# Seven products for eight, in one more column group of w_down and in half of the gate's v columns

## The chip, the cores and the metric

The kernel runs on one core of one Trainium2 chip. The metric is device time in microseconds. The kernel before took 2023.43 us as the median of three runs (2023.22 to 2023.98).

## What is computed

Two layers over 256 tokens of width 2048, all in fp32. Cut to what matters here:

```
for l in range(DEPTH):                                  # DEPTH = 2
    h = rms_norm(x, norm1_g[l])
    z = h @ w_in[l]                                     # 2048 x 5120
    q, k, v, gu, gv = jnp.split(z, splits, axis=-1)     # 1024 columns each
    q, k = rotary(q), rotary(k)
    attn = dilated_attention(q, k, v)                   # 8 heads of 128
    gm = chunked_gmlp(gelu(gu), gelu(gv), ...)          # 8 groups of 128: layer norm of gv, 128x128 mixing
    x = x + concat([attn, gm]) @ w_out[l]               # 2048 x 2048
    h2 = rms_norm(x, norm2_g[l])
    x = x + square(relu(h2 @ w_up[l])) @ w_down[l]      # 2048 x 8192, 8192 x 2048
```

`gv` is "the gate's v half" of the change. Its layer norm (one per group of 128 columns) feeds a 128x128 product per group, the spatial product.

## The kernel before

**Precision.** Every large product runs on TensorE as three passes of a rounded type: weights and activations are each split into `hi` (the rounded value) and `lo` (the rest), and hi·hi, lo·hi and hi·lo are summed in PSUM. A weight tile ("sub") is 1024 numbers for each of 128 partitions. SP's queue loads it as `raw` (7 buffers); ScalarE (ACT) rounds it to `hi` at line 168 (6 buffers); VectorE (DVE) takes `lo = raw - hi` at line 178 (6 buffers); PE multiplies. The high and low parts of an activation pair come from `to_half` (ACT line 646, DVE line 649).

**Three forms of product.** `transposed` (line 410) keeps the weights stationary and moves 256 tokens: 24 matmuls of 256 columns for one sub. `natural` (lines 470 to 472) keeps the activations stationary and moves 512 weight columns: 12 matmuls of 512 columns for one sub; v and gv come out of it with tokens on the partitions. `fast` (line 440) is a Strassen-Winograd step over 1024 rows and 512 columns, with 2x2 blocks of weights and of activations: seven block products for eight. It has two steps (p = 0, 1) of 42 matmuls of 256 columns. A step takes two loads and makes four subs of them: `Top` (half a tile), `Bottom`, and two of sums, `upper` and `lower`; before `upper` stands on ACT, DVE makes two differences of the raw tiles, and before `lower` two more (lines 219 to 224). It also needs the activation sums, which `sums` (line 800) makes in place on DVE from `inner`, the unsplit activations, and `parts` turns into hi and lo.

**Order.** The schedule is written out by hand: `steps` is a list, and a loop at the end of the program walks it. `done` counts the subs used up. Ahead of a step's matmuls the loop emits the `hi` of subs up to done+5 and the `lo` of subs up to done+4. `soon(n, f)` puts f in front of the matmuls of the step that is n subs later. `later(n, cost, f)` puts f in a queue that is emptied, within a budget of 1.2 us, at the end of each entry of `steps`; an entry made by `mark` has no matmuls, and the queue is emptied behind it as well. The five engines each work through their own list in the order in which it was emitted.

**The first half of a layer.** v (16 natural steps); then k and q of two heads at a time, k0 q0 k1 q1 k2 q2 k3 q3, four transposed steps each; then gv (16 natural steps), gu (16 transposed steps), and w_out. When a k or q block is complete, `after_qk` turns it (ACT lines 577 and 578, DVE lines 579 to 581). Two steps behind a q block stand `scores` (PE lines 593 and 596; DVE lines 602 and 604; exponentials on ACT line 606), then `normalise` (DVE line 611, ACT line 614), `turn` (PE line 622) and `values` (PE lines 635 and 637). gv is scaled on ACT (line 660), goes through gelu (ACT 490, DVE 493, ACT 494, DVE 667), then statistics (DVE 677, 680), then `layer_norm` on GpSimd (POOL, line 690). `spatial` (PE line 699) stands behind the first step of the second, third and fourth gu blocks and of w_out.

**The second half.** Step groups e = 0 to 8: group e computes the e-th eighth of w_up (16 transposed steps of 24 matmuls) and, against the eighth before it, w_down, some column groups of 512 with `fast`, at the places in `ORDER` and `USUAL`:

```
ORDER = {1: ((7, 10), (13, 14)), 6: ((12, 15), (2, 3), (7, 8)), 7: ((7, 10), (2, 3)), 8: ()}
USUAL = ((7, 9), (2, 3), (13, 14))
```

Each pair is the two steps of one column group, as step numbers inside group e. Group 1 of steps therefore has two column groups by seven products, and the third goes through `transposed`.

Of the kernel before, what the change touches and what calls it, by code (L numbers as in the profile page):

```python
# [61 lines left out]

ORDER = {1: ((7, 10), (13, 14)), 6: ((12, 15), (2, 3), (7, 8)), 7: ((7, 10), (2, 3)), 8: ()}
FINAL = (7, 7, 6)
# [3 lines left out]
HALVES = 5  # L68
BEHIND, BETWEEN = 2, 1
D_SCORES, D_NORM, D_TURN, D_VALUES = 2, 1, 3, 2  # L70

# [20 lines left out]
def trunk(ctx: ExitStack, tc: tile.TileContext, layout, xT, consts, gains, w, b_sp, w_sp, out):  # L92
# [8 lines left out]
    pacc = ctx.enter_context(tc.tile_pool(name="pacc", bufs=1, space=bass.MemoryType.PSUM))  # L101
    paux = ctx.enter_context(tc.tile_pool(name="paux", bufs=4, space=bass.MemoryType.PSUM))

# [31 lines left out]
    def acc_bank(i=None, of=4):  # L135
# [3 lines left out]
        return pacc.tile([P, 512], F32, name=f"acc{i}", tag=f"acc{i}")  # L139

    def aux_bank():
        return paux.tile([P, 512], F32, name="aux", tag="aux")

# [222 lines left out]
    def sums_ready():  # L366
        run_until(lambda: summed[0])
# [45 lines left out]

    def fast(name, l, row0, col0, tiles, slots, fresh, last, done):

# [5 lines left out]
        for p in range(2):  # L421
# [3 lines left out]
            def mm(p=p, top=top, bottom=bottom, upper=upper, lower=lower):  # L425
                if p == 0:
                    o.extend(slots())
                half = tiles[0][0]
                sums_ready()
                extra = sum_parts[0]  # L430
                left, right = slice(0, 256), slice(256, 512)

                calls = []

                def product(n, a, lower_rows, tt, b, cols):
                    for k in range(2):
                        xh, xl = (a[:, 4 * lower_rows + 2 * p + k, i, tt * P:(tt + 1) * P] for i in range(2))
                        hi, lo = b.hi[:, k, cols], b.lo[:, k, cols]
                        for j, (lhs, rhs) in enumerate(((xh, hi), (xh, lo), (xl, hi))):
                            calls.append(lambda k=k, j=j, lhs=lhs, rhs=rhs: pe.matmul(  # L440
                                o[n], lhsT=lhs, rhs=rhs, start=(p == 0 and k == 0 and j == 0 and n in fresh),
                                stop=(n in last and p == 1 and k == 1 and j == 2), skip_group_check=True))
# [32 lines left out]
    def mark(fn):  # L475

        steps.append((None, fn, None))

    def from_hs(k):
# [38 lines left out]
    def layer(l, n1, n2, n3, last):  # L518
# [27 lines left out]
        if l:  # L546
            mark(start)
        mix_a, mix_g = [None], [None]
        qk = {}
# [107 lines left out]
        def after_gv(c, ps):  # L657
            z, u = t32("gz", [2, 512], tag="tmpB"), t32("gu", [2, 512], tag="tmpA")
            for tt in range(2):
                act.activation(z[:, tt, :], ps[tt], AF.Copy, scale=n1.half[:, tt:tt + 1])  # L660

            def then(u, z):
# [6 lines left out]

            gelu(z, u, then)  # L670

        def stats(g0):
# [10 lines left out]
        def layer_norm(g0):  # L683
            y, mv = par["y"], par["mv"]
            r = t32("lr", [2, 4])
            rsqrt(nc.gpsimd, r, mv[:, :, g0:g0 + 4, 1], 1.0, LN_EPS, [2, 4])
            for g in range(4):
                for tt in range(2):
                    yg = y[:, tt, (g0 + g) * P:(g0 + g + 1) * P]
                    nc.gpsimd.tensor_scalar(yg, yg, mv[:, tt, g0 + g, 0:1], r[:, tt, g:g + 1],  # L690
                                            op0=OP.subtract, op1=OP.mult)
            par["normed"] += 4
# [47 lines left out]
        hook(base + d + 6, rope)  # L740
        hook(base + d + 8, shift)
        for j in range(4):
            transposed("w_in", l, 0, KC, AW + j * 256, 256, from_hs, lambda c, ps, j=j: after_qk("k", j, ps))
            transposed("w_in", l, 0, KC, j * 256, 256, from_hs, lambda c, ps, j=j: after_qk("q", j, ps))
        natural("w_in", l, 4 * AW, AW, after_gv)
        transposed("w_in", l, 0, KC, 3 * AW, AW, from_hs, after_gu)
# [34 lines left out]
        def after_up(e):  # L781
            def f(c, ps):
# [7 lines left out]
                act.activation(z, z, AF.Square)  # L790
                to_half(hid[e][0], c // P, z, True)
                if c == 768:
                    summed[0] = False
                    if e == 0:
                        new_shared(F32R)
                        sum_parts[0] = shared[0].rearrange("p (k h t) -> p k h t", k=NH, h=2)
                    later(1, 1.5, sums)
            return f

        def sums():  # L800

            a11, a12, a21, a22 = (inner[:, 4 * k:4 * k + 4, t * P:(t + 1) * P] for t in range(2) for k in range(2))
            vec.tensor_tensor(a22, a21, a22, op=OP.add)
            vec.tensor_tensor(a21, a11, a21, op=OP.subtract)
            vec.tensor_tensor(a11, a22, a11, op=OP.subtract)
            vec.tensor_tensor(a12, a12, a11, op=OP.subtract)

# [4 lines left out]
            for k in range(0, 8, 2):  # L812
                later(0, 0.6, lambda k=k: parts(k))

# [33 lines left out]

        def halves(bank):
            return [bank[:, 0:256], bank[:, 256:512]]  # L850

        held = []
# [17 lines left out]
        def put(e, g, r):  # L870

            src = stage[:, r] if g else stage_one
            nc.gpsimd.dma_start(far[g][:, r], src, **({} if e == max(g, 1) else {"accum_op": OP.add}))  # L873

# [38 lines left out]
        for e in range(9):  # L913
# [3 lines left out]
            if e < 8:  # L917
                up = collect(transposed, "w_up", l, 0, KC, e * 1024, 1024, from_hs, after_up(e), of=2)
            if e:
                w = 512 * len(ORDER.get(e, USUAL))  # L920
                hidden = [hid[e - 1]]
                down = collect(transposed, "w_down", l, (e - 1) * 1024, 8, w, D - w, from_tiles(hidden, NH),
                               lambda c, ps, e=e, w=w: after_down(e, (c + w) // P, ps),
                               apart=last and e == 8, of=2 if e < 8 else 4,
                               cols=None if e < 8 else [c * P for c in LAST])
                for g, at in enumerate(ORDER.get(e, USUAL)):
                    banks = []
                    quick += zip(at, collect(fast, "w_down", l, (e - 1) * 1024, 512 * g, hidden,
                                             (lambda g=g, banks=banks: slots_other(g, banks)) if g else slots_first,
# [146 lines left out]
```

## Time and profile before

| | |
|---|---|
| median of three runs | 2023.43 us |
| profiled execution | 2023.7 us, its span 2021.9 us |
| granted TensorE clock, mean | 0.997 |
| PE / DVE / ACT / POOL busy | 99% / 78% / 60% / 8% |
| HBM | 206 GB/s over the span, DMA engines busy 50 to 90% of a slice |

Busy time of PE is the union of matmuls that overlap each other, so the pace of a stage is read from start to start in the chain of waits, not from the mean duration of a matmul (277 ns for 256 columns). DVE and ACT instructions start some 0.1 us before the one ahead of them is reported as ended. In an answer by lines or by time, `x48` is a count, the first number a start or a sum, and the arrow in square brackets is what ended the idle time before the instruction.

### The profile page before, as it was taken

Reading aid. Unit: us, or ns where it says so; the run is one execution under the profiler, and the core shown is the slowest. Engines: PE = TensorE matmul, PEld = TensorE weight load, DVE = VectorE, ACT = ScalarE, POOL = GpSimd, SP = SyncE. Lnnn points to the kernel's source line nnn. Section 1 sums busy time; section 2 is a strip of 40 time slices with the busy share of each in tenths; the row PEclk is TensorE's granted clock in tenths of the full one; section 3 lists DMA queues with packets and bytes.
Section 4 is the critical chain, followed back from the end, with each engine's and each line's share of the span. In section 5 each row is a group of like instructions: output and inputs, shape, how many; then the busy total and the mean of one; then the engine's idle time right before and its main releaser. Section 6 shows DMA issues by size and latency. Waiting matters only on the chain.

```text
span 2021.9 us, 40716 instructions
## 1 busy us (share of the span) xinstructions
PE 2009.5 (99%) x16810; PEld 1973.4 (98%) x16810; DVE 1579.8 (78%) x1954; ACT 1221.2 (60%) x1613; POOL 156.2 (8%) x200
## 2 busy tenths in 40 slices
PE   9999999999999999999999999999999999999997
PEld 8998999999999999999989989999999999999997
DVE  7566766688888898898856667667888898888985
ACT  7565455566566666665645654556666666667653
POOL 0002300000001000100000032000000000010000
PEclk9999999999999999999999999999999999999998
DMA  9555556566678776866664555565676776777662
GB/s 330 192 167 167 187 189 202 174 229 204 222 219 239 240 225 203 249 215 215 201 215 158 168 187 188 188 199 179 217 229 208 228 236 216 239 220 241 212 215 81
DMA packets 126442, 419.26 MB, mean 207 GB/s; under 512 B 14128, under 2 KB 22064, under 8 KB 126256
## 3 DMA queue, kind: packets, MB, share of 16 engines
q1 hardware_dynamic: 110800, 389.86, 57.2%
q0 software_dynamic: 14304, 23.86, 6.5%
q8 instruction: 131, 2.15, 0.4%
q10 hardware_dynamic: 1152, 2.94, 0.4%
q14 instruction: 55, 0.45, 0.1%
HBM read 394.58 MB, written 22.02 MB: 206 GB/s over the span
## 4 chain that ended last, share of the span: by engine, by line
PE 99%; DVE 0%; ACT 0%; issue 0%; DVEq 0%
PE acc L410 70%; PE acc L440 10%; PE aux L440 8%; PE acc L470 3%; PE acc L472 3%; PE acc L471 3%; PE aux L699 0%; PE aux L635 0%; PE aux L593 0%; PE aux L622 0%; PE aux L994 0%; DVE x L1038 0%; PE aux L596 0%; PE aux L637 0%; PE acc L846 0%; PE aux L539 0%
## 5 line engine op out<-in xcount | busy, mean ns | idle before, releaser
L168 ACT ACTIVATE hi<-raw 128x1024 fp32r<-128x1024 f32 (+1 forms) x817 | 836.9, 1050 | 487.5 <-DVE raw L220 216.2
L178 DVE TENSOR_TENSOR lo<-raw,hi 128x1024 fp32r<-128x1024 f32 (+1 forms) x817 | 965.3, 1214 | 143.4 <-ACT hi L168 140.4
L410 PE MATMUL acc<-hs,hi 128*128 128x256 f32 x5632 | 985.9, 277 | 0.0
L410 PEld LDWEIGHTS acc<-hs,hi 128*128 128x128 f32 x5632 | 857.9, 188 | 0.4 <-issue 0.2
L410 PE MATMUL acc<-hs,lo 128*128 128x256 f32 x2816 | 778.0, 276 | 0.0
L410 PEld LDWEIGHTS acc<-hs,lo 128*128 128x128 f32 x2816 | 528.7, 188 | 0.4 <-issue 0.2
L410 PE MATMUL acc<-half,hi 128*128 128x256 f32 x2688 | 462.2, 276 | 0.0
L410 PEld LDWEIGHTS acc<-half,hi 128*128 128x128 f32 x2688 | 406.7, 188 | 0.0
L410 PE MATMUL acc<-half,lo 128*128 128x256 f32 x1344 | 371.0, 276 | 0.0
L410 PEld LDWEIGHTS acc<-half,lo 128*128 128x128 f32 x1344 | 252.3, 188 | 0.0
L873 POOL DMA_DIRECT2D far<-ar x92 | 74.2, 816 | 1164.4 <-ACT ar L876 563.9
L440 PE MATMUL acc<-hi,shared 128*128 128x256 f32 x768 | 138.4, 276 | 0.0
L440 PEld LDWEIGHTS acc<-hi,shared 128*128 128x128 f32 x768 | 119.2, 188 | 0.0
L440 PE MATMUL aux<-hi,half 128*128 128x256 f32 x528 | 110.6, 276 | 0.0
L440 PE MATMUL acc<-lo,shared 128*128 128x256 f32 x384 | 106.0, 276 | 0.0
L649 DVE TENSOR_TENSOR half<-ar,half 128x512 fp32r<-128x512 f32 x72 | 49.8, 691 | 68.6 <-ACT half L646 68.6
L470 PE MATMUL acc<-hi,hs 128*128 128x512 f32 x256 | 101.8, 398 | 0.0
L472 PE MATMUL acc<-hi,hs 128*128 128x512 f32 x256 | 100.6, 393 | 0.0
L471 PE MATMUL acc<-lo,hs 128*128 128x512 f32 x256 | 100.3, 392 | 0.0
L440 PEld LDWEIGHTS aux<-hi,half 128*128 128x128 f32 x528 | 87.2, 188 | 0.0
L440 PE MATMUL aux<-hi,shared 128*128 128x256 f32 x448 | 80.7, 276 | 0.0
L510 DVE TENSOR_TENSOR x<-x,acc 128x512 f32<-128x512 f32 (+1 forms) x49 | 33.1, 675 | 59.1 <-PE acc L410 57.3
(150 smaller groups left out, 1955.3 us busy)
## 6 DMA issues: line engine op xcount, KB each, us to landing
raw<-in_w SPq DMA_DIRECT2D x731, 512.0 KB, 4.7
far<-ar POOLq DMA_DIRECT2D x60, 256.0 KB, 8.3
far<-ar POOLq DMA_DIRECT2D x32, 128.0 KB, 4.3
ar<-far POOLq DMA_DIRECT2D x12, 256.0 KB, 9.7
raw<-in_w SPq DMA_DIRECT2D x10, 256.0 KB, 5.1
x<-in_xT SPq DMA_DIRECT2D x7, 256.0 KB, 5.9
out<-x SPq DMA_DIRECT2D x7, 256.0 KB, 3.1
shared<-in_b_sp ACTq DMA_DIRECT2D x2, 512.0 KB, 7.7
```

The source lines that it names most:

```text
L168: act.activation(self.h[:, j * m:(j + 1) * m], self.raw[:, j * m:(j + 1) * m], AF.Copy)
L178: vec.tensor_tensor(lo[:, r], self.raw[:, r], self.h[:, r].bitcast(F32), op=OP.subtract)
L410: pe.matmul(o, lhsT=lhs, rhs=xs[:, rhs, :], start=(first and j == 0), stop=(last and j == 2), skip_group_check=True)
L440: calls.append(lambda k=k, j=j, lhs=lhs, rhs=rhs: pe.matmul(o[n], lhsT=lhs, rhs=rhs, start=(p == 0 and k == 0 and j == 0 and n in fresh), ...
L470: pe.matmul(ps, lhsT=xh, rhs=hi, start=(k0 + k == 0), stop=False)
L471: pe.matmul(ps, lhsT=xh, rhs=lo, start=False, stop=False)
L472: pe.matmul(ps, lhsT=xl, rhs=hi, start=False, stop=(k0 + k == KC - 1))
L510: vec.tensor_tensor(xj, xj, ps[j][:, 0:S] if alone else pair(ps)[:, j, :], op=OP.add)
L649: vec.tensor_tensor(t[:, c:c + 2, 1, :], src, t[:, c:c + 2, 0, :].bitcast(F32), op=OP.subtract)
L873: nc.gpsimd.dma_start(far[g][:, r], src, **({} if e == max(g, 1) else {"accum_op": OP.add}))
```

## The change

Two things, each in both layers. First, `ORDER[1]` gets a third pair: in step group 1 the third column group (512 columns of w_down, 1024 rows) now goes by `fast`, at steps 13 and 14, and the other two move to 9, 11 and to 5, 6. For that, half of the activation sums are made earlier (`sums([0])` behind the second block of group 0, whose blocks are taken in another order), and the partial results that wait in DRAM are written first in group 1.

Second, the first 512 columns of gv, over both halves of the 2048 rows, go by `fast`. Their four steps stand among the k and q steps: at plain steps 4 and 7 (in q0) for the upper rows, at 15 (in q1) and 23 (in q2) for the lower. Their activation sums are made from x times gain by `seven_sums` (8 ACT, 4 DVE instructions) and `seven_parts` (four times one ACT and one DVE instruction); for the lower rows these stand in marks in front of plain steps 8 to 12. The result stays in two accumulator banks and two auxiliary banks of PSUM until `gather` adds the seven products up on DVE. Meanwhile k and q use two accumulator banks and the small score block an accumulator bank. The other 512 columns stay natural (8 steps), and the gelu of the first half starts inside them. `layer_norm` of the first half moves from POOL to DVE.

```
-ORDER = {1: ((7, 10), (13, 14)), 6: ((12, 15), (2, 3), (7, 8)), 7: ((7, 10), (2, 3)), 8: ()}
+ORDER = {1: ((9, 11), (5, 6), (13, 14)), 6: ((12, 15), (2, 3), (7, 8)), 7: ((7, 10), (2, 3)), 8: ()}
+SEVEN, AGAIN = ((4, 7), (15, 23)), 8
...
-            s1, s0 = aux_bank(), aux_bank()
+            s1, s0 = aux_bank(), acc_bank(1 - bank_at[0]) if aux_held else aux_bank()
...
+        def seven_sums(rows):
+            if "sums" not in seven:
+                f = tp.tile([P, 2, NH, S], F32, name="plain", tag="half", bufs=2)
+                seven["plain"] = [f[:, i, :, :] for i in range(2)]
+                seven["sums"] = tp.tile([P, NH, 2, S], F32R, name="half", tag="half", bufs=2)
+            f = seven["plain"][rows]
+            for k in range(NH):
+                c = NH * rows + k
+                act.activation(f[:, k, :], x[:, c, :], AF.Copy, scale=g_all[:, n1.g, c:c + 1])
+            strassen_sums(f, 0, 4)
+
+        def seven_parts(rows, k):
+            to_half(seven["sums"], k, seven["plain"][rows][:, k:k + 2, :])
...
+        def gather(o):
+            z = t32("gz", [2, 512], tag="tmpB")
+            p1, p2, p3, p5, p7, p6, p4 = o
+            c11, c12, c21, c22 = (z[:, tt, h * S:(h + 1) * S] for tt in range(2) for h in range(2))
+            act.activation(c12, p1, AF.Copy)
+            vec.tensor_tensor(c11, c12, p2, op=OP.add)
...
+            for tt in range(2):
+                act.activation(z[:, tt, :], z[:, tt, :], AF.Copy, scale=n1.half[:, tt:tt + 1])
...
-            rsqrt(nc.gpsimd, r, mv[:, :, g0:g0 + 4, 1], 1.0, LN_EPS, [2, 4])
+            e = nc.gpsimd if g0 else vec
+            rsqrt(e, r, mv[:, :, g0:g0 + 4, 1], 1.0, LN_EPS, [2, 4])
...
+        hook(base + 13, lambda: seven_sums(0))
+        for k in range(0, NH, 2):
+            hook(base + 14 + k // 2, lambda k=k: seven_parts(0, k))
...
-        natural("w_in", l, 4 * AW, AW, after_gv)
...
+        for i, one in enumerate(plain):
+            if quick.get(i):
+                steps.append(quick[i])
+            if i == AGAIN:
+                mark(lambda: seven_sums(1))
+            if AGAIN < i <= AGAIN + 4:
+                mark(lambda k=2 * (i - AGAIN - 1): seven_parts(1, k))
+            steps.append(one)
+        late = collect(natural, "w_in", l, 4 * AW + 512, 512, lambda c, ps: soon(1, lambda: after_gv(512, ps)))
+        for i, one in enumerate(late):
+            if i == 6:
+                mark(lambda: gate_half(0, seven["z"]))
+            steps.append(one)
```

In the changed program lines 168, 178, 410 and 440 have become 173, 183, 415 and 443; `scores` is at 608 and 611 (PE), 617 and 619 (DVE); the turning of q and k at 592 to 596; `spatial` at 768.

**First place: PE, layer 0, from the last matmul of q0 to the scores of heads 0 and 1.** `acc` is the accumulator of a block, `hi_…`/`lo_…` a weight sub, `hs` the activations, `ar` the tile that holds q and k. Before:

```order
L410 MATMUL acc2_703<-hs_85,hi_632 128x256
L410 MATMUL acc3_829<-hs_85,hi_662 128x256 [waits Activation_49]
...
L410 MATMUL acc3_829<-hs_85,hi_697 128x256 [waits Activation_49]
...
L410 MATMUL acc3_829<-hs_85,hi_697 128x256
L593 MATMUL aux_884<-ar_80 128x256 [waits DVE_49,PE_49]
L593 MATMUL aux_884<-ar_80 128x256
L596 MATMUL aux_885<-ar_80 128x128 [waits PE_49]
```

and now:

```order
L415 MATMUL acc0_793<-hs_85,hi_850 128x256
L415 MATMUL acc1_999<-hs_85,hi_880 128x256 [waits Activation_49]
...
L415 MATMUL acc1_999<-hs_85,hi_880 128x256
L608 MATMUL aux3_1026<-ar_80 128x256 [waits DVE_49]
L608 MATMUL aux3_1026<-ar_80 128x256
L611 MATMUL acc0_1027<-ar_80 128x128 [waits PE_49,Activation_49]
L611 MATMUL acc0_1027<-ar_80 128x128
L415 MATMUL acc1_999<-hs_85,hi_926 128x256
```

Two subs of k1 (662, 697) stood between q0 and its scores; now it is one (880), since the marks in front of plain steps 8 and 9 empty the queue as well.

**Second place: DVE, layer 0, from the turning of q0 to the first fast step in q1.** `mx`, `den` and `ar` belong to the attention, `plain` and `half` to the activation sums. Before:

```order
L579 TENSOR_TENSOR ar<-acc_703,cosR 128x512
L580 TENSOR_TENSOR ar<-ar,sinR 128x512
L581 TENSOR_TENSOR ar<-ar 128x512
L178 TENSOR_TENSOR lo<-raw,hi 128x1024 x2
L602 SCALAR_TENSOR_TENSOR ar<-aux,con 128x512
L604 TENSOR_REDUCE mx<-ar 128x2
L602 SCALAR_TENSOR_TENSOR ar<-aux,con 128x256
L604 TENSOR_REDUCE mx<-ar 128x2
L178 TENSOR_TENSOR lo<-raw,hi 128x1024
L611 RECIPROCAL den<-den 128x4
L178 TENSOR_TENSOR lo<-raw,hi 128x1024
L579 TENSOR_TENSOR ar<-acc_829,cosR 128x512
```

Now, behind the same three instructions (lines 594 to 596), first

```order
L485 TENSOR_TENSOR plain<-plain 128x4x128
L486 TENSOR_TENSOR plain<-plain 128x4x128
L487 TENSOR_TENSOR plain<-plain 128x4x128
L488 TENSOR_TENSOR plain<-plain 128x4x128
L183 TENSOR_TENSOR lo<-raw,hi 128x1024
L664 TENSOR_TENSOR half<-plain,half 128x2x256
L617 SCALAR_TENSOR_TENSOR ar<-aux_1026,con 128x512
L619 TENSOR_REDUCE mx<-ar 128x2
L617 SCALAR_TENSOR_TENSOR ar<-acc_1027,con 128x256
L619 TENSOR_REDUCE mx<-ar 128x2
L183 TENSOR_TENSOR lo<-raw,hi 128x1024
L664 TENSOR_TENSOR half<-plain,half 128x2x256
```

and then

```order
L626 RECIPROCAL den<-den 128x4
L183 TENSOR_TENSOR lo<-raw,hi 128x1024
L664 TENSOR_TENSOR half<-plain,half 128x2x256
L196 TENSOR_TENSOR lo<-raw,hi 128x512
L594 TENSOR_TENSOR ar<-acc_999,cosR 128x512
L595 TENSOR_TENSOR ar<-ar,sinR 128x512
L596 TENSOR_TENSOR ar<-ar 128x512
L664 TENSOR_TENSOR half<-plain,half 128x2x256
L183 TENSOR_TENSOR lo<-raw,hi 128x1024
L224 TENSOR_TENSOR raw<-raw 128x2x256
L225 TENSOR_TENSOR raw<-raw 128x2x256
```

Behind these stand lines 228 and 229 and the `lo` of `upper` and `lower`. Between the turning of q0 and that of k1 there were four `lo` of whole subs and the scores; now there are three, one of a half sub (line 196, `Top`), the scores, four sums and three parts.

**Third place: DVE, layer 0, from the second half's gelu to the first gu block.** `shared` holds the gated values, `mv` their statistics. Now:

```order
L507 SCALAR_TENSOR_TENSOR ar<-ar 128x1024
L183 TENSOR_TENSOR lo<-raw,hi 128x1024
L745 BN_STATS bst<-shared 128x6 x8
L748 BN_AGGR mv<-bst 128x2 x8
L686 SCALAR_TENSOR_TENSOR shared<-ar 128x2x512
L183 TENSOR_TENSOR lo<-raw,hi 128x1024
L349 TENSOR_SCALAR rv<-mv 128x8
L353 TENSOR_SCALAR rt<-rv 128x8
...
L759 TENSOR_SCALAR shared<-shared,mv,lr 128x128 x8
L183 TENSOR_TENSOR lo<-raw,hi 128x1024
L776 SCALAR_TENSOR_TENSOR ar<-acc_2212,nR 128x512
```

Before, at the same place:

```order
L493 SCALAR_TENSOR_TENSOR ar<-ar 128x1024
L178 TENSOR_TENSOR lo<-raw,hi 128x1024
L667 SCALAR_TENSOR_TENSOR shared<-ar 128x2x512
L178 TENSOR_TENSOR lo<-raw,hi 128x1024 x2
L677 BN_STATS bst<-shared 128x6 x8
L680 BN_AGGR mv<-bst 128x2 x8
L178 TENSOR_TENSOR lo<-raw,hi 128x1024
L707 SCALAR_TENSOR_TENSOR ar<-acc_2085,nR 128x512
```

The statistics and the layer norm of the first half have come to stand among the gu steps, on DVE, ahead of the first gu block's own work.

More of the change, by code (lines that the diff above doesn't have):

```diff
@@ L139, in acc_bank @@
         return pacc.tile([P, 512], F32, name=f"acc{i}", tag=f"acc{i}")
+    aux_at, aux_held = [3], set()
     def aux_bank():
-        return paux.tile([P, 512], F32, name="aux", tag="aux")
+        i = next(j % 4 for j in range(aux_at[0] + 1, aux_at[0] + 5) if j % 4 not in aux_held)
+        aux_at[0] = i
+        return paux.tile([P, 512], F32, name=f"aux{i}", tag=f"aux{i}")
     class Sub:
@@ L791, in f, with sums @@
                 to_half(hid[e][0], c // P, z, True)
+                if e == 0 and c == 512:
+                    new_shared(F32R)
+                    sum_parts[0] = shared[0].rearrange("p (k h t) -> p k h t", k=NH, h=2)
+                    later(1, 1.0, lambda: sums([0]))
                 if c == 768:
                     summed[0] = False
[L794 to L797, printed above, removed]
-            return f
[L800 to L806, printed above, removed]
+                    later(1, 1.5, lambda: sums([0, 1] if e else [1]))
+            return f
+        def sums(ps):
+            strassen_sums(inner, 2 * ps[0], 2 * len(ps))
             def parts(k):
@@ L812, in sums @@
             for k in range(0, 8, 2):
-                later(0, 0.6, lambda k=k: parts(k))
+                if k % 4 // 2 in ps:
+                    later(0, 0.6, lambda k=k: parts(k))
         def combine(place, c, banks, o=None):
@@ L917, in layer @@
             if e < 8:
[L918 removed]
+                up = collect(transposed, "w_up", l, 0, KC, e * 1024, 1024, from_hs, after_up(e), of=2,
+                             cols=None if e else (0, 512, 256, 768))
             if e:
```

70 lines of the change are left out of this document (56 added, 14 removed).

## The prediction

> **What bounds it now.** I read the page first: busy times, the chain that ended last by engine, then PE's waits (engine, line, what is waited for: us, times, longest).
>
> ```profile
> PE 2009.5 (99%) x16810; PEld 1973.4 (98%) x16810; DVE 1579.8 (78%) x1954; ACT 1221.2 (60%) x1613; POOL 156.2 (8%) x200
> PE 99%; DVE 0%; ACT 0%; issue 0%; DVEq 0%
> PE aux L328 <- DVE nr L354: 1.2, 1, 1.2
> PE aux L994 <- DVE warm L990: 1.1, 1, 1.1
> ```
>
> PE waits 2.3 us in 2021.9. So matmuls taken away shorten the end one for one, and any wait that the change brings lengthens it one for one. Next come the stages that it touches, in the view by windows (length, then busy time and count of PE, PEld, DVE, ACT, POOL, then clock, DMA share, GB/s): k and q of layer 0, its gu blocks, a whole up/down group of layer 1.
>
> ```profile
> 51.60:149.30 97.70, 97.70 (x832) 96.22 (x831) 61.66 (x81) 55.13 (x92) 0.00 (x0) 1.00 0.55 176
> 198.00:247.90 49.90, 49.90 (x443) 49.90 (x442) 38.76 (x61) 26.89 (x33) 21.06 (x25) 1.00 0.53 170
> 1529.00:1612.00 83.00, 83.00 (x733) 83.00 (x733) 72.78 (x82) 54.73 (x70) 7.08 (x10) 1.00 0.70 226
> ```
>
> DVE is at 63% in k/q, 78% in gu, 88% in the up/down group, and PE waits in none. The k/q and gu stages have the room on average; the change fills it in bursts.
>
> **What it removes from PE.** Pace is read from start to start: the chain (start, length) for 256 columns, the timeline for 512.
>
> ```profile
> 1107.84 10.90 PE acc L410 x96
> 1500.47 4.54 PE aux L440 x40
> 16.20 0.39 PE L470 MATMUL acc<-hi,hs 128*128 128x512 f32 x1
> 31.31 0.39 PE L470 MATMUL acc<-hi,hs 128*128 128x512 f32 x1
> ```
>
> 10.90/96 and 4.54/40 are both 113.5 ns. Between the last two rows lie 66 matmuls, 15.11/66 = 228.9 ns. Per layer the v half loses 8 × 12 = 96 matmuls of 512 (21.97 us) and gains 4 × 42 = 168 of 256 (19.07): −2.90. Group 1's third column group goes from 96 to 84 of 256: −1.36. Together −4.26 a layer, **−8.5 us**.
>
> A rule speaks against this. Were narrow matmuls to carry a fixed price that wide ones don't, 168 narrow could cost more than 96 wide. The Trainium skill, "TensorE: Matmul & The Clock Gate", section "Back-to-back issue gap", gives for a stream 81 ns at 128 columns and 131 at 512; an estimate from it is 98 at 256, and by that the v half would cost 3.8 us more a layer, the group 1.2 less, and the sum below would end at 2039. The trace does not agree: 2 × 113.5 = 227.0 stands against 228.9, with no fixed price in it. I give that outcome no chance.
>
> **What it adds.** Groups by form (total busy, mean ns; then idle time before):
>
> ```profile
> L168 ACT ACTIVATE hi<-raw 128x1024 fp32r<-128x1024 f32 x807 | 830.7, 1055 | 485.8 <-DVE raw L220 216.2 <-PE acc L410 149.4 <-PE acc L472 49.3
> L178 DVE TENSOR_TENSOR lo<-raw,hi 128x1024 fp32r<-128x1024 f32 x807 | 958.7, 1220 | 139.3 <-ACT hi L168 136.2
> L191 DVE TENSOR_TENSOR lo<-raw,hi 128x512 fp32r<-128x512 f32 x76 | 52.0, 684 | 2.1 <-ACT hi L186 2.1
> L220 DVE TENSOR_TENSOR raw<-raw 128x512 f32<-128x512 f32 x76 | 52.6, 692 | 2.6
> L646 ACT ACTIVATE half<-ar 128x512 fp32r<-128x512 f32 x72 | 45.4, 630 | 2.0
> L649 DVE TENSOR_TENSOR half<-ar,half 128x512 fp32r<-128x512 f32 x72 | 49.8, 691 | 68.6 <-ACT half L646 68.6
> ```
>
> A step by seven products turns two loads into 0.68 + 3 × 1.22 + 4 × 0.69 = 7.1 us of DVE instead of 2.4, and 0.63 + 3 × 1.06 = 3.8 of ACT (a half-width row is L646) instead of 2.1.
>
> *Group 1* thereby becomes what the third window shows: up plus three groups by seven and one by eight, 83 us with no wait. Its activation sums are made earlier in parts, and eight more writes go to DRAM from POOL, nearly idle there. I cost it at nothing beyond its gain; uncovered, a late pair of differences would cost 0 to 2 us a layer.
>
> *First rows of the v half* (plain steps 4 and 7, in q0): 2 × 4.7 us of DVE over 16 us in which about 37% of it is free, besides sums made a stage earlier. I put the waits at 0; the tightest `lo` I find has about 0.3 us to spare, so 0 to 1.
>
> *Second rows: q0's end to step 15.* Here the marks stack a burst. Rows of the same work in layer 1 (timeline, and three pieces of the chain):
>
> ```profile
> 262.27 0.91 ACT L287 ACTIVATE hs<-x,cols 128x256 fp32r<-128x256 f32 x2 [2.33 <-DVE x L510]
> 1076.33 0.59 ACT L578 ACTIVATE ar<-acc 64x512 f32<-64x512 f32 x1
> 1076.95 0.69 DVE L579 TENSOR_TENSOR ar<-acc,cosR 128x512 f32<-128x512 f32 x1 [4.37 <-ACT ar L578]
> 1078.27 0.69 DVE L581 TENSOR_TENSOR ar<-ar 128x512 f32<-128x512 f32 x1
> 1081.06 0.86 PE aux L593 x4
> 1081.92 0.44 PE aux L596 x4
> 1081.96 0.69 DVE L602 SCALAR_TENSOR_TENSOR ar<-aux,con 128x512 f32<-128x512 f32 x1 [0.72 <-PE aux L593]
> 1083.41 0.51 ACT L606 ACTIVATE ar<-ar,mx 128x256 f32<-128x256 f32 x1 [3.97 <-DVE mx L604]
> 1084.08 1.21 DVE L178 TENSOR_TENSOR lo<-raw,hi 128x1024 fp32r<-128x1024 f32 x1
> 1085.18 1.04 ACT L168 ACTIVATE hi<-raw 128x1024 fp32r<-128x1024 f32 x1
> 1086.13 1.48 ACT L614 ACTIVATE ar<-ar,den 128x256 f32<-128x256 f32 x4
> 93.19 0.65 PE aux L622 x6
> ```
>
> Two transposed steps of 24 × 113.5 = 2.72 us lie ahead of the scores at 1081.06, so q0 ended at 1075.61. Set that to 0 in the changed order. ACT turns q until 1.3 (row 1076.33), DVE until 3.3 (1076.95 and 1078.27: three of 0.66). The scores now stand one step behind q0, at 2.7: **wait 0.7**. ACT's eight gains go on to 4.7 (two take 0.91 with the tail, 0.41 from start to start), DVE's four sums, at 0.70, to 7.5. Behind these DVE has one `lo` (8.6), a part (9.2) and only then the scores, four operations in 2.12 (1081.96 to 1084.08): 11.3. Before, they came at once. ACT's exponentials (1.77, 1083.41 to 1085.18) end at 12.4, a `hi` and a part's high half at 14.0. DVE: `lo` 12.5, part and reciprocal 14.8, `lo` 15.9. ACT: scaling (1.4) 16.2, `Top` 16.7, part 17.3, `hi` 18.2, and only then the turning of k1, which PE finished at about 13.6, to 19.5. DVE: part 18.0, `Top` 18.6, turning 21.4, last part 22.0, `Bottom` 23.2, four differences 25.9; then `upper` 27.2, `lower` 28.4, each `lo` behind its `hi`.
>
> PE, from 2.7, takes 0.7 of wait, 1.3 of scores (0.86 + 0.44), 0.65 of transposes (93.19) and seven steps behind the first: it reaches step 15 at 21.7 and, unhindered, would end its 4.77 at 26.5. The products from `upper` and `lower` end it; with the last `lo` at 28.4 and the matmuls behind it the step ends at 29.8: **wait 3.3**. The next plain step's `lo` comes at 30.2: **0.35**. Four subs of lead, 4 × 2.72 = 10.9 us, are used up here, since DVE has 22 us of work between 1.3 and 28.4 and stands 5 us for ACT and PE. Together 4.3 a layer; DVE's instructions ready sooner would leave the 0.7, and two orders gone wrong by one `lo` each would make it 6.4.
>
> *Third rows* (step 23, in q2): no marks near it. The queue has room, and I find no wait; the result is gathered five steps later, 14 operations against a window with a third of DVE free.
>
> *Gate.* The first half's gelu moves forward into the natural steps, and its layer norm goes to DVE, ahead of the first gu work. The rows:
>
> ```profile
> 1105.23 0.43 PE aux L635 x2
> 1105.66 0.22 PE aux L637 x2
> 197.37 1.38 ACT L660 ACTIVATE ar<-acc,nhalf 128x512 f32<-128x512 f32 x2 [1.00 <-PE acc L472]
> 198.78 1.06 ACT L490 ACTIVATE ar<-ar 128x1024 f32<-128x1024 f32 x1
> 199.88 1.23 DVE L493 SCALAR_TENSOR_TENSOR ar<-ar 128x1024 f32<-128x1024 f32 x1 [4.95 <-ACT ar L490]
> 202.24 1.32 DVE L667 SCALAR_TENSOR_TENSOR shared<-ar 128x1024 f32<-128x1024 f32 x1
> 205.75 1.63 DVE L677 BATCH_NORM_STATS2 bst<-shared 128x6 f32<-128x128 f32 x8
> 207.30 0.62 DVE L680 BATCH_NORM_AGGREGATE mv<-bst 128x2 f32<-128x6 f32 x8
> 1018.61 0.16 DVE L344 TENSOR_SCALAR rv<-aux 128x2 f32<-128x2 f32 x1 [3.46 <-PE aux L320]
> 1020.86 3.50 DVE L178 TENSOR_TENSOR lo<-raw,hi 128x1024 fp32r<-128x1024 f32 x3
> 57.97 2.16 DVE L543 SCALAR_TENSOR_TENSOR shared<-aux,cols,shared 128x128 f32<-128x128 f32 x8 [2.67 <-PE aux L539]
> ```
>
> Set 0 at q3's end. PE gets through the last values at 26.6 (eight natural steps of 12 × 228.9, 22.0; scores 1.3; transposes 0.65; two rounds of values, each twice 0.43 + 0.22); behind them come a part's two halves (0.6, 0.65), the first half's y (1.2), 29.1. The second half's scaling waits for that buffer (1.4), then Square (1.1), 31.6; DVE's inner step, a `lo`, the statistics (1.55 + 0.55), y, a `lo`, and the root (2.25, from 1018.61 to 1020.86): 40.6. The layer norm on DVE isn't in the trace; nearest is 0.26 an operation (row 57.97). PE reaches the spatial product at 26.6 + 5 × 2.72 = 40.2 and its fourth matmul, 0.66 later, needs the fourth, at 41.7: **wait 0.85**, of 0 (POOL's free, or y 1 us sooner) to 1.6.
>
> **Sum.** −8.5 + 2 × 4.3 + 2 × 0.85 = **+1.8**. The profiled execution took 2023.7, its span 2021.9; 0.27 over the median. So span 2023.7, execution 2025.5, against the median **2025.2**. With the low ends of the waits, 2 × 0.7, it is −7.1: 2016.3. With the high, 2 × (6.4 + 1.6), +7.5: 2030.9.
>
> **Rivals.** *The lead holds (faster).* If ACT doesn't delay DVE in the burst, step 15 costs nothing: 1 us a layer or less remains, −6.5: 2016.9. For it: the third window's DVE does 88% without a wait, with its own bursts of differences. Against: there nothing stands ahead of them that waits for PE; here scores and turning do.
>
> *DVE falls behind in gu (slower).* DVE has 38.8 of 49.9 us there (second window); the change adds statistics 2.1, root 2.25, layer norm 2.1 and a displaced y and `lo` of 2.4 to 47.7, or 96%. If the last layer norm ends over 3 us after PE has reached the spatial product, each following `lo` is as late: 3 us a layer more, 2031.2. Against: the lead of 10.9 us, and ACT is at 54%.
>
> *It doesn't do what it says*: the changed order holds the counted matmuls, so no chance for that.
>
> **Chances.** Within 0.2% (4 us, about what a measurement here tells from no change): 0.47, own range 2020 to 2027.5. Faster 0.30; slower 0.23, which takes in step 15 dearer by an order more. The range 2017 to 2029.5 leaves out a third of the faster case and somewhat under half of the slower, 0.2 together.
>
> **What would show it.** PE's waits in the changed profile: 0.7 us twice at the first scores (line 608), some 3.3 twice at the step by seven in q1 (line 443), 0.85 twice at the spatial product (line 768), and none in group 1. PE's busy count falls by 192 matmuls of 512 columns and rises by 312 of 256. I am wrong if line 443 waits under 1 us a layer, or if waits stand at plain steps of gu.

## The result, and the profile after

The changed kernel takes 2070.01 us (median of 6, 2061.71 to 2074.86), the one before 2023.62: a ratio of 1.0227, 95% interval 1.0207 to 1.0248. It is 46 us slower. The time lies 40 us above the top of the predicted range.

The page of the changed kernel, first its busy times and its chain by engine, then PE's waits:

```profile
PE 2048.3 (99%) x16930; PEld 2016.8 (98%) x16930; DVE 1661.9 (80%) x2108; ACT 1262.1 (61%) x1695; POOL 137.0 (7%) x166
PE 92%; DVE 4%; ACT 2%; issue 1%; DMA 0%; SPq 0%; DVEq 0%; ACTq 0%
PE acc L443 <- DVE lo L183: 2.9, 3, 1.1
PE acc L443 <- ACT hi L173: 1.7, 2, 0.9
PE aux L608 <- DVE ar L596: 1.2, 2, 0.6
PE aux L768 <- DVE shared L759: 0.8, 2, 0.4
```

The new waits sum to 6.6 us in this view, and they stand at the lines that the prediction names. PE is as busy as before, 99%, yet 39 us longer. So the time is neither in the waits nor in more matmuls: the matmuls themselves take longer. The view by windows shows it for 300 us in the step groups of each layer, where both programs run the same mixture. First the kernel before, then the changed one (length, then busy time and count of PE, PEld, DVE, ACT, POOL, then clock, DMA share, GB/s):

```profile
500.00:800.00 300.00, 300.00 (x2645) 300.00 (x2645) 262.31 (x297) 197.73 (x250) 26.52 (x32) 1.00 0.72 225
1500.00:1800.00 300.00, 300.00 (x2646) 300.00 (x2645) 261.86 (x296) 197.77 (x250) 26.25 (x32) 1.00 0.72 225
```

```profile
500.00:800.00 300.00, 300.00 (x2547) 300.00 (x2546) 252.14 (x282) 193.22 (x241) 27.59 (x32) 1.00 0.71 216
1500.00:1800.00 300.00, 300.00 (x2550) 300.00 (x2549) 254.37 (x285) 192.33 (x240) 26.50 (x31) 1.00 0.72 221
```

The granted clock is 1.00 in all four, PE is busy for all of the 300 us, and it starts 2645 matmuls before and 2547 now: 113.4 ns and 117.8 ns each. The busy time cannot show this; the count in a window does. On the page only the mean duration of one matmul moves with it, from 277 ns (line 410) to 280 ns (line 415).

Where the pace turns is seen in PE's timeline of the changed kernel (start, busy time), in step group 1 of layer 0 and at the first transposes of group 6:

```profile
435.39 0.28 PE L415 MATMUL acc<-hs,hi 128*128 128x256 f32 x1
435.77 0.38 PE L443 MATMUL acc<-hi,half 128*128 128x256 f32 x1
...
888.45 0.28 PE L415 MATMUL acc<-half,hi 128*128 128x256 f32 x1
888.57 0.60 PE L937 MATMUL acc<-con,ar 128*128 128x128 f32 x4
888.92 0.37 PE L415 MATMUL acc<-half,hi 128*128 128x256 f32 x1
```

Between 435.39 and 435.77 lies 0.38 us where 0.11 would do: PE waited 0.27 us. From there on it starts a matmul of 256 columns every 117.8 ns, for 453 us, until the four narrow transposes at 888.57; behind them it is 113.4 ns again. These transposes stand among the last steps of group 6, where the third column group is finished: the first of the group's four steps of w_down lies ahead of them. Where the expectations below speak of group 8, these are meant. In layer 1 the same happens from 1462 to 1915. Counted from start to start, some 10,000 matmuls of the profiled execution run at 117.8 ns, against some 230 before; 9,800 x 4.44 ns = 43.5 us.

The chain of waits of the kernel before has the slow pace too, in one longer stretch of each layer, between the scores of heads 0 and 1 and their transposes:

```profile
77.97 2.61 PE acc L410 x23
80.57 0.86 PE aux L593 x4
81.44 0.44 PE aux L596 x4
81.88 11.31 PE acc L410 x96
93.19 0.65 PE aux L622 x6
93.84 3.19 PE acc L410 x28
```

11.31/96 is 117.8 ns; 2.61/23 ahead of it and 3.19/28 behind it are 113.5 and 113.9. The two paces could have been read before the change was run.

The books of the profiled executions, 2069.4 against 2023.7: matmuls -8.5, waits from start to start +10.1, a halved clock in layer 1 +1.7 (last section), slow pace +43.5. That is 46.8 of 45.7.

### The profile page after: what moved, and what is told of

Read it like the earlier page. It is cut to its first block, busy times and chain, and to the rows that moved or that the text cites. A ratio compares the mean times of both kernels' runs of the same rounds, so it can differ in the third digit from the quotient of the medians.

```text
span 2067.6 us, 41171 instructions
## 1 busy us (share of the span) xinstructions
PE 2048.3 (99%) x16930; PEld 2016.8 (98%) x16930; DVE 1661.9 (80%) x2108; ACT 1262.1 (61%) x1695; POOL 137.0 (7%) x166
## 4 chain that ended last, share of the span: by engine, by line
PE 92%; DVE 4%; ACT 2%; issue 1%; DMA 0%; SPq 0%; DVEq 0%; ACTq 0%
PE acc L415 64%; PE acc L443 12%; PE aux L443 8%; PE acc L473 2%; PE acc L475 2%; PE acc L474 2%; DVE lo L183 1%; ACT hi L173 1%; PE aux L768 0%; PE aux L650 0%; ACT plain L714 0%; DVE raw L225 0%; DVE raw L228 0%; DVE raw L229 0%; DMA raw<-in_w 0%
## 5 line engine op out<-in xcount | busy, mean ns | idle before, releaser
L183 DVE TENSOR_TENSOR lo<-raw,hi 128x1024 fp32r<-128x1024 f32 (+1 forms) x829 | 981.9, 1217 | 131.7 <-ACT hi L173 127.3
L415 PE MATMUL acc<-hs,hi 128*128 128x256 f32 x5632 | 1011.5, 280 | 0.0
L415 PEld LDWEIGHTS acc<-half,hi 128*128 128x128 f32 x2560 | 390.4, 188 | 0.0
L415 PE MATMUL acc<-half,lo 128*128 128x256 f32 x1280 | 356.3, 278 | 0.0
L443 PE MATMUL acc<-hi,shared 128*128 128x256 f32 x832 | 154.5, 279 | 0.0
L443 PE MATMUL aux<-hi,half 128*128 128x256 f32 x608 | 129.6, 280 | 0.0
L443 PEld LDWEIGHTS aux<-hi,half 128*128 128x128 f32 x608 | 101.2, 188 | 0.0
L443 PE MATMUL acc<-hi,half 128*128 128x256 f32 x480 | 94.8, 280 | 1.9 <-ACT hi L173 1.7
L443 PE MATMUL aux<-lo,half 128*128 128x256 f32 x304 | 85.0, 280 | 0.0
L443 PEld LDWEIGHTS acc<-hi,half 128*128 128x128 f32 x480 | 77.5, 188 | 2.7 <-ACT hi L173 2.1
```

The source lines that it names most:

```text
L183: vec.tensor_tensor(lo[:, r], self.raw[:, r], self.h[:, r].bitcast(F32), op=OP.subtract)
L415: pe.matmul(o, lhsT=lhs, rhs=xs[:, rhs, :], start=(first and j == 0), stop=(last and j == 2), skip_group_check=True)
L443: calls.append(lambda k=k, j=j, lhs=lhs, rhs=rhs: pe.matmul(o[n], lhsT=lhs, rhs=rhs, start=(p == 0 and k == 0 and j == 0 and n in fresh), ...
```

## Experiments

The theory after the result: PE has two paces for the same stream of 256-column matmuls. A wait inside the stream, however short, can put it into the slow one, and it stays there until something else interrupts the stream. The rivals: the pace belongs to the changed program (its banks of PSUM, its order), or a wait costs just what it lasts and the time is elsewhere.

**One part alone, twice.** The v half's part without group 1's:

```
-ORDER = {1: ((9, 11), (5, 6), (13, 14)), ...
+ORDER = {1: ((7, 10), (13, 14)), ...            # and sums, order of group 0, writes as before
```

> The v half's part of the change alone: group 1 of the steps (its column groups, sums and writes) as before. Pace theory: no wait in group 1, so no slow pace in groups 1 to 7 (33.7 us less) but the one in k, q, gv and gu as in the changed kernel (11 us), and 2.7 us of matmuls and 0.8 of waits come back: about 2038. Rival, the new pool of banks gives the slow pace in the groups: 2070 or more.

Measured: 2036.32 us, ratio 1.0065 (1.0050 to 1.0080). And group 1's part without the v half's (the kernel before with the new `ORDER[1]`, the sums in two parts, the order of group 0 and the writes):

> Group 1's part of the change alone, the v half as before. Pace theory: 24 matmuls fewer (2.7 us), waits of 0.4 us a layer in group 1, and the slow pace from there to group 8, 33.7 us: about 2055. If the short wait doesn't come up without the v half's part: 2021. Rival, the slow pace comes with the v half's banks: 2021 to 2022.

Measured: 2054.89 us, ratio 1.0156 (1.0141 to 1.0172). Both came out as the pace theory worked them out, within 2 us. Group 1's part, which takes 2.7 us of matmuls away, costs 31.6 us by itself. The bank pool of the v half's part is not in that kernel, and the v half's part alone, which has it, starts 2646 and 2645 matmuls in the two windows of 300 us, as the kernel before does. So the pool is not the cause of the slow pace in the groups. The window of group 1's part in layer 0:

```profile
500.00:800.00 300.00, 300.00 (x2549) 300.00 (x2549) 251.46 (x282) 193.82 (x244) 27.62 (x32) 1.00 0.72 219
```

The wait behind it, in the timelines of ScalarE and PE of the same kernel, and then in the view of waits, where it stands with the weight loads (PEld), for this kernel and for the changed one (there the Relu is line 880):

```profile
428.48 1.06 ACT L168 ACTIVATE hi<-raw 128x1024 fp32r<-128x1024 f32 x1 [3.34 <-DVE raw L220]
429.93 1.06 ACT L168 ACTIVATE hi<-raw 128x1024 fp32r<-128x1024 f32 x1 [0.39 <-DVE raw L224]
430.90 0.58 ACT L795 ACTIVATE ar<-acc 128x512 f32<-128x512 f32 x1
...
431.15 0.28 PE L410 MATMUL acc<-hs,hi 128*128 128x256 f32 x1
431.53 0.39 PE L440 MATMUL acc<-hi,half 128*128 128x256 f32 x1
...
PEld acc L440 <- ACT ar L795: 0.6, 2, 0.3
PEld acc L443 <- ACT ar L880: 0.6, 2, 0.3
```

Line 795 is the Relu that reads the finished block's accumulator. It stands in ScalarE's list behind two roundings that waited 3.34 and 0.39 us for VectorE's differences, ends at 431.48, and PE's next matmul by seven, which writes into that bank, starts at 431.53 instead of 431.26. The rows of the matmuls alone do not list this wait; those of the weight loads name it, once in each layer.

**A wait put into the kernel before.** Two matmuls more, into a free bank that ScalarE reads in between:

```
+        def stall():
+            b = acc_bank(2)
+            for j in range(2):
+                pe.matmul(b[:, 0:S], lhsT=hs[:, 0, 0, 0:P], rhs=hs[:, 0, 0, :], start=True, stop=True)
+                if j == 0:
+                    act.activation(warm[:, 0:1], b[:, 0:1], AF.Copy)
```

> The kernel before with two matmuls of 256 columns more behind the ninth plain step of group 1, in both layers, into one free bank; ScalarE reads one column of that bank in between, so that TensorE waits once, 1 to 2 us, for ScalarE. Pace theory: from there to the transposes of group 8 TensorE runs at 117.8 ns, about 3500 matmuls a layer x 4.45 ns = 15.6 us, in both layers 31, and with the waits 2056 to 2060. Rival, a wait costs what it lasts: 2025.5 to 2028.

Measured, eight times: 2025.8, 2025.9 and 2026.2; 2043.7, 2044.1 and 2044.3; 2061.4 and 2062.5. The granted clock is 0.997 or 0.998 in all eight. The median, 2043.88, says little. The time is that of the waits alone, or 18 us more, or 36 more. The profiled execution was one of 2044, and its rows show what the 18 us are (PE's timeline around the wait in layer 0 and in layer 1, and the two windows):

```profile
406.12 0.28 PE L915 MATMUL acc<-hs 128*128 128x256 f32 x1
407.19 0.39 PE L915 MATMUL acc<-hs 128*128 128x256 f32 x1 [0.80 <-ACT warm L917]
...
1425.78 0.28 PE L915 MATMUL acc<-hs 128*128 128x256 f32 x1
1426.86 0.38 PE L915 MATMUL acc<-hs 128*128 128x256 f32 x1 [0.80 <-ACT warm L917]
...
500.00:800.00 300.00, 300.00 (x2547) 300.00 (x2547) 251.91 (x281) 194.12 (x242) 26.41 (x32) 1.00 0.70 216
1500.00:1800.00 300.00, 300.00 (x2645) 300.00 (x2645) 260.98 (x293) 198.97 (x251) 27.08 (x33) 1.00 0.73 227
```

The same program, the same wait of 0.97 us (1.07 and 1.08 less a matmul's time), once in each layer: behind the one PE runs at 117.8 ns to the transposes of group 6 (4075 matmuls x 4.44 ns = 18.1 us), behind the other at 113.4. So a wait does not always bring the slow pace. It lets the pace be drawn anew, and here slow came up 7 times in 16, read from the eight times at 18 us each; only the profiled execution has rows. I had expected it always; that was wrong. Nor is it an even draw at every place: the four runs of group 1's part lie within 2054.50 to 2055.38, so its wait brought the slow pace in both layers each time.

**A row of narrow matmuls.** Four transposes of a constant into a free bank, in group 1 of the changed kernel:

> The changed kernel with four transposes of 128 columns more on TensorE (of a constant, into a free bank) behind the ninth plain step of step group 1, in both layers; nothing else differs. Pace theory: after the 0.26 us wait in the first steps by seven of group 1 TensorE goes on at 117.8 ns per matmul of 256 columns instead of 113.3, and only a row of narrow matmuls brings it back. 7642 matmuls ran slowly there in both layers; all but some 350 of them become fast again: 7300 x 4.45 ns = 32 us less, for 1 us of transposes: about 2039. Rival, the changed program's banks or order make that pace: it comes back at once, 2071. The rows should show 113.3 ns from behind the transposes to group 8.

Measured: 2067.48 us, ratio 1.0227 (1.0204 to 1.0249): no gain. The expectation had the place wrong, for the wait of group 1 is at its step 13 (435.77 above), behind the row. But the trace tells more than that, in two windows of 16 us ahead of the row and behind it, and the row itself in the timeline:

```profile
400.00:416.00 16.00, 16.00 (x144) 16.00 (x143) 13.57 (x16) 9.86 (x12) 1.88 (x3) 1.00 0.69 233
418.00:434.00 16.00, 16.00 (x138) 16.00 (x137) 15.05 (x17) 9.44 (x11) 0.00 (x0) 1.00 0.72 229
...
416.54 0.60 PE L1003 MATMUL acc<-con 128*128 128x128 f32 x4
```

Ahead of the row 144 matmuls start in 16 us, behind it 138, with no wait between (a window counts two or three at its edges with the rest; from start to start it is 113.4 and 117.8 ns). It stays so to the transposes of group 6, and layer 1 does the same. A row without any wait turned fast into slow. "Narrow matmuls bring it back" fell here; "an interruption draws the pace anew" stands.

**Rows of many lengths**, on group 1's part alone, in groups 2 to 7:

```
+                if 2 <= e <= 7 and i == 11:
+                    hook(len(steps) - 1, lambda k=((1, 2, 3, 5, 6, 7), (4, 8, 10, 12, 16, 24))[l][e - 2]: narrow(k))
```

> Group 1's part alone (slow from step 13 of group 1 on), and in each of groups 2 to 7, behind plain step 11, a row of 128-column transposes of a constant into a free bank: 1, 2, 3, 5, 6, 7 of them in layer 0 and 4, 8, 10, 12, 16, 24 in layer 1. If narrow rows bring the fast pace back by their number, the pace turns to 113.3 behind some of these rows and stays there; if a row only draws the pace anew by its timing, it goes up and down without an order in the number; if only what follows the row decides, none of them changes it and the time is that of the part alone with 12 us of transposes, about 2066.

One run: 2050.22 us. The windows between the rows of layer 1 (rows of 4, 8, 10 and 12 transposes lie between them):

```profile
1442.00:1524.00 82.00, 82.00 (x699) 82.00 (x698) 71.62 (x81) 54.70 (x70) 7.06 (x10) 1.00 0.72 230
1526.00:1608.00 82.00, 82.00 (x724) 82.00 (x724) 72.68 (x82) 54.08 (x68) 7.68 (x9) 1.00 0.71 223
1610.00:1695.00 85.00, 85.00 (x723) 85.00 (x723) 72.88 (x82) 53.95 (x67) 7.67 (x9) 1.00 0.69 215
1697.00:1779.00 82.00, 82.00 (x725) 82.00 (x724) 72.39 (x82) 53.81 (x67) 7.68 (x9) 1.00 0.70 221
1782.00:1867.00 85.00, 85.00 (x724) 85.00 (x723) 72.50 (x82) 54.66 (x69) 10.34 (x12) 1.00 0.74 217
```

Slow, fast, slow, fast, slow: 4 turned slow into fast, 8 fast into slow, 10 slow into fast, 12 fast into slow; 16, behind the last window, left it slow. In layer 0, 1 left the pace slow, 2 made it fast, 3 and 5 left it fast, 6 made it slow. (The rows of 7 and 24 stand 0.4 us ahead of transposes of the kernel's own and cannot be read apart from them.) The pace does not follow the size of the number. But there is a pattern that the expectation did not foresee: the rows of 1, 3 and 5 left the pace as it was, those of 2, 4, 6, 8, 10 and 12 turned it, whichever it was, and 16 broke the series. One execution does not make that a rule; rows of four come back below.

**The row behind the wait.** Four transposes in group 2 of the changed kernel:

> The changed kernel with four transposes of 128 columns behind plain step 11 of group 2, in both layers: behind the wait of group 1, not ahead of it as in x1_narrow. Pace theory with the pace drawn anew by a row (in x7_rows four transposes at this place turned 117.8 into 113.4): some 720 matmuls of a layer stay slow in groups 1 and 2, 3100 become fast, 2 x 3100 x 4.45 ns = 27.6 us less, 1 us of transposes: 2043. If the row is drawn slow: 2071. Rival, the changed program's banks make the pace: 2071 as well, but then no row at all would change it.

Measured: 2044.89 us, ratio 1.0100 (1.0085 to 1.0116): 25 us less than the changed kernel, for 0.9 us more work on PE. The windows of layer 0 ahead of the row and behind it:

```profile
450.00:520.00 70.00, 70.00 (x596) 70.00 (x595) 61.02 (x69) 46.98 (x61) 5.67 (x8) 1.00 0.76 243
530.00:800.00 270.00, 270.00 (x2381) 270.00 (x2381) 235.38 (x265) 179.81 (x228) 26.92 (x31) 1.00 0.74 227
```

117.4 and 113.4 ns, and the same in layer 1. It is the changed program with its banks and its order, so neither by itself makes the pace. The row turned slow into fast here, and the same row in group 1 turned fast into slow; with those of the kernels below, all nine rows of four that were added with no wait ahead of them turned the pace that they met.

**The wait taken away.** In group 1's part alone, the third column group one step later, which gives the late Relu 2.7 us:

```
-ORDER = {1: ((9, 11), (5, 6), (13, 14)), ...
+ORDER = {1: ((9, 11), (5, 6), (14, 15)), ...
```

> Group 1's part of the change alone, with its third column group one plain step later (14, 15 for 13, 14); the v half as before. In the run of that part alone TensorE waited 0.27 us at step 13, since ScalarE's Relu of the block before, which frees the bank, stood behind roundings that waited for VectorE. One step later that Relu has 2.7 us more. Pace theory: no wait, so no slow pace: 2023.3 - 24 x 113.4 ns = 2020.6. If the row of matmuls by seven itself brings the slow pace, 2055 again; if the wait moves to the next bank, 2055 too, with a row of waits at another line or step.

Measured: 2020.47 us (11 runs), ratio 0.9986 (0.9977 to 0.9995), where 24 matmuls of 113.4 ns were to give 2020.6. PE's waits are those of the kernel before, no weight load waits for line 795 any more, and 2646 matmuls start in each window of 300 us. One step's place in a table is worth 34 us here.

**The whole change without its waits**, in three tries. First the second rows at steps 19 and 23, their sums behind steps 10 to 14, the first spatial product a step later, and (14, 15) as above:

> The whole change with four places moved: the third column group of group 1 at 14, 15; the second rows of the v half at plain steps 19 and 23 (not 15, 23); their sums and parts behind plain steps 10 to 14 without emptying the queue a second time, so that the scores of heads 0 and 1 stand two steps behind q0 again; and the first spatial product one step later. Nothing is left out. By the sums on record the waits were 0.9, 3.5 and 0.65 us a layer at these places. Pace theory, all of them gone: 2023.3 - 8.5 = 2015, plus what slow pace the scores bring until the next transposes (1 us in the kernel before, up to 11 if it lasts through k, q and gu): 2015 to 2026. Rival, the matmuls by seven in the v half cost more than their pace says: over 2026 without waits.

Measured: 2031.47 us, ratio 1.0040 (1.0027 to 1.0052). A wait of 2.3 us stayed at step 19 and the step behind it in layer 0, and the pace, drawn slow at the head products that end gv, lasted through gu in both layers: 12.0 us of slow pace in all. Then the gains and sums spread out, steps 20 and 24, and a row of four transposes early in gu:

> As x6_all_late, with three more places moved: ScalarE's eight gains for the second rows' sums in pairs behind plain steps 3 to 6, the sums behind 8 and their parts behind 9, 10, 12 and 13; the second rows' steps at 20 and 24; and one row of four 128-column transposes behind the second gu step, in both layers. Nothing is left out. Pace theory: in x6_all_late 4.1 us of waits and 11 us of slow pace more than before stood against 8.5 us saved; without the waits, and with the pace drawn anew (fast) early in gu, 2023.3 - 8.5 + 0.9 (the rows) + 1 = 2016 to 2018. If the row in gu draws the slow pace again, 2026. Rival, the v half's matmuls by seven are dearer than their pace says: over 2020 with no wait and no slow pace in the rows.

Measured: 2020.17 us (11 runs), ratio 0.9986 (0.9977 to 0.9994). It beats the kernel before by 3.4 us, though 2 to 4 less than expected. The rows make gu fast in both layers; in k and q the pace stayed slow for all of layer 0 (4.3 us of slow pace in all, against 1.0 before), and one wait was left behind step 20:

```profile
PE acc L415 <- DVE lo L183: 1.9, 2, 1.0
```

-8.5 for the matmuls, +3.3 for pace, +2.3 for this wait from start to start and +0.9 for the rows make -2.0; its profiled execution took 2.2 less than that of before. So the books close with the v half's matmuls by seven at what their pace says. Last, a step later again, and a row in k and q:

> As x8_all_spread, with the second rows' steps one plain step later (21, 25) and one more row of four 128-column transposes behind plain step 14, in both layers. Nothing is left out. In x8_all_spread one wait of 1.25 us a layer was left, at the plain step ahead of step 20, and a slow pace through k and q worth 3.3 us. Pace theory: without them, and with 0.9 us for the new rows, 2020.2 - 2.7 - 2.5 + 0.9 = 2016. If the wait only moves on with the step, and the row at step 14 is drawn slow, 2020 to 2022.

Measured: 2026.16 us, ratio 1.0014 (1.0005 to 1.0023), a miss. ("Ahead of step 20" in this expectation should read behind it.) The slow pace fell to 2.9 us, but the wait only moved to step 21, and PE now waits at more places:

```profile
PE aux L443 <- DVE lo L183: 2.4, 2, 1.4
PE aux L637 <- DVE ar L739: 0.9, 2, 0.5
PE aux L637 <- DVE ar L741: 0.5, 2, 0.3
```

Line 637 is the transposes of the attention, held up by the gathering of the v half (lines 739 and 741) that has come to stand ahead of them.

## Why the prediction was wrong

**Matmuls: right.** 192 of 512 columns fell away and 312 of 256 came, and two kernels bear out 113.4 ns: group 1's part without its wait (2020.47 for 2020.6), and the whole change with its places moved, whose books close (-2.0 for -2.2).

**The waits: right in three places of four, and nearly in size.** From start to start, less a matmul's own time:

| place | predicted, a layer | measured |
|---|---|---|
| first scores, line 608 | 0.7 | 0.9 and 0.9 |
| step 15 by seven and the step behind it | 3.65 | 3.5 and 2.8 |
| spatial product, line 768 | 0.85 | 0.6 and 0.6 |
| group 1 | 0 (0 to 2) | 0.4 and 0.4 |
| sum of both layers | 10.3 | 10.1 |

The rows for step 15 in layer 0:

```profile
106.92 0.39 PE L443 MATMUL acc<-hi,hs 128*128 128x256 f32 x2
107.95 0.39 PE L443 MATMUL acc<-lo,hs 128*128 128x256 f32 x1 [0.64 <-DVE lo L183]
...
109.24 0.28 PE L443 MATMUL acc<-hi,half 128*128 128x256 f32 x1
110.37 0.38 PE L443 MATMUL acc<-hi,half 128*128 128x256 f32 x1 [0.85 <-ACT hi L173]
111.87 0.38 PE L443 MATMUL acc<-lo,half 128*128 128x256 f32 x1 [1.12 <-DVE lo L183]
```

107.04 to 107.95 is 0.80 over a matmul's time, 109.24 to 111.87 is 2.4 over two. The sum of these two terms, matmuls and waits, is +1.8 by the prediction and +1.6 in the trace; that it comes so close is in part luck, for step 15 and the spatial product were put too high and the first scores and group 1 too low. (The "seven steps behind the first" on the way to step 15 are six; the 21.7 is worked out with six.)

**The step that failed** is the first one: "any wait that the change brings lengthens it one for one". It rests on the pace, "10.90/96 and 4.54/40 are both 113.5 ns", read in two places and taken for all. In fact a wait also throws the pace open, and what follows it can run 4.44 ns a matmul slower until the next interruption. How much that costs depends on how far off the next interruption is, not on how long the wait lasts. In group 1 that is the first transposes of group 6, 3840 matmuls on: 17 us a layer for 0.4 us of waiting. This is why the cheapest item of the ledger, "I cost it at nothing", was the dearest, 34 us of the 46 (2 x 3840 matmuls x 4.44 ns), and why both rivals and the range, which were all made of waits, lay far off.

**Group 1** failed in a second way. By its comparison with the third window (DVE at 88% with no wait) no weight would come late, and none did. The wait that came was for a bank of PSUM: its reader, a Relu, stood in ScalarE's list behind roundings that waited for VectorE's differences. The bounds of 0 to 2 us covered the wait, and "a late pair of differences" is at its root, but it reached PE by a way that the prediction did not look at.

**The rival of a carried-on delay in gu** did not come: the gu waits are 0.6 us a layer, with no others at its plain steps.

## What to carry to other kernels

Read the pace of a saturated engine by counts in equal windows, over the whole span and not in two places: if the same instruction has two paces at the same clock, price what would switch between them before pricing any wait. Where the long stretch runs undisturbed, a change that adds even 0.3 us of waiting at its start can cost fifty times that, as it did here; move the work until the wait is gone rather than accept it as small. And when an engine gives back a buffer late, look at what stands ahead of the reader in its own list.

## What the runs showed of the hardware

**Two paces.** At a granted clock of 1.00, matmuls of 256 columns with a weight load each follow one another every 113.4 ns or every 117.8 ns, and each pace keeps itself up over thousands of them (3840 in a row in the changed kernel). Matmuls of 512 columns have two paces as well. In a slow stretch of the changed kernel 22 of them take 5.13 us, and behind the head products and scores that end it 45 take 10.31 us, 233.2 ns and 229.1 ns each (PE's timeline):

```profile
174.66 0.40 PE L474 MATMUL acc<-lo,hs 128*128 128x512 f32 x1
...
179.79 0.40 PE L475 MATMUL acc<-hi,hs 128*128 128x512 f32 x1
...
182.88 0.40 PE L474 MATMUL acc<-lo,hs 128*128 128x512 f32 x1
...
193.19 0.39 PE L474 MATMUL acc<-lo,hs 128*128 128x512 f32 x1
```

A wait of 0.27 us or more, a row of transposes, the scores or the values can each leave either pace behind. Behind the inserted wait the draw differed from run to run of one program (7 of 16 slow). Behind a row without a wait it depended on the pace ahead of it and on the place. The added rows of four with no wait ahead of them turned whichever pace there was. The kernel's own four transposes in group 6 left the fast pace in both layers of all twelve profiled executions, having met the slow one nine times and the fast one fifteen. What in TensorE settles it stays open; no run here looked inside it. The six runs of the changed kernel lie 13 us apart and those of the kernel before 0.8; that its shorter stretches are drawn anew from run to run would explain this, but only one of the six was profiled.

**A halved clock.** In layer 1 of the changed kernel, the waits of 1.02 and 1.39 us at step 15, within 2.6 us, were followed by a stretch at half clock:

```profile
1129.00:1133.00 4.00, 2.03 (x13) 1.63 (x14) 3.85 (x6) 2.38 (x3) 0.00 (x0) 1.00 0.00 0
1133.00:1138.00 5.00, 5.00 (x31) 5.00 (x31) 4.52 (x5) 5.00 (x7) 0.00 (x0) 0.66 0.84 229
```

PE was busy for 2.03 of 4 us, and in the 5 us behind that the mean granted clock was 0.66: 0.34 x 5, some 1.7 us lost. Single matmuls started 213 ns apart there. In layer 0 the same two waits had no such sequel. The Trainium skill, "TensorE: Matmul & The Clock Gate", Part 1, puts the halving down to an idle window of about 3.4 us, and says that this window runs freely. The trace fits the second in that the same gaps met the halving once and missed it once; it differs from the first in that 2.4 us of waiting within 2.6 us were enough here.
